# Gated linear attention: decays to the chunks' ends taken in the exponential's bias, a subtraction taken into scans, and GpSimd's elementwise work moved to VectorE

## The chip, the cores and the metric

One core of a Trainium2 chip runs the whole program in one launch. The metric is device time in microseconds (us) from the first to the last instruction of an execution; the time before is the median of three.

## What is computed

Two transformer blocks on 256 tokens of width 1024 in fp32. The first block has three token mixers on one input projection (attention, gated linear attention, a Hyena convolution) and a mixture of experts; the second has four feed-forward layers, a pooling mixer and a sparse attention. The change lies in the gated linear attention (four heads, chunks of 64 tokens, a forward and a backward direction), and in one line of the convolution:

```python
def gla_log_decay(a_low, w_a2, b_a):
    z = (a_low @ w_a2 + b_a)
    return to_heads(jax.nn.log_sigmoid(z) / GLA_TAU, GLA_HEADS)          # GLA_TAU = 16

def gla_chunked(q, k, v, log_a, s0):             # latent tokens, per chunk of 64
    cum = jnp.cumsum(log_a, axis=3);  cum_last = cum[:, :, :, -1:, :]
    q_dec = q * jnp.exp(cum);         k_inv = k * jnp.exp(-cum)
    k_to_end = k * jnp.exp(cum_last - cum)
    att = where(tril, q_dec @ k_inv.T, 0);       o_intra = att @ v
    chunk_state = k_to_end.T @ v;                chunk_decay = jnp.exp(cum_last)
    # states are scanned over the chunks; o = o_intra + q_dec @ state

def gla_final_state(k, v, log_a):                # context tokens, one run of 256
    cum = jnp.cumsum(log_a, axis=2)
    return jnp.einsum('bhld,bhlv->bhdv', k * jnp.exp(cum[:, :, -1:, :] - cum), v)
```

The context's final state is the latent tokens' first one. The backward direction is the same on flipped tokens.

## The kernel before

**Layout.** Every head has one tile of 128 partitions by 512 columns: the forward direction's 64 key channels are partitions 0 to 63 (`lo`), the backward's 64 to 127 (`hi`); columns 0 to 255 are the latent tokens, 256 to 511 the context's. The work order on every engine is a scheduler's, made from the order in which the code records it and its priorities; each engine then runs its own list in order. PE's list runs almost without a break, since the split matmuls of the projections (`in_tiles`, L1354) make up most of the work: each tile is 24 matmuls (`mm3`, lines 169, 171, 173), for which ScalarE rounds the weights (`wh`, line 158) and VectorE subtracts the rest (`wl`, line 159), three tiles ahead at most.

**`Gla.decays` (L645).** A generator that `in_tiles` steps between the projection's tiles. Per head a matmul (L659), then ScalarE's absolute value and exponential into a tile `e` of the ring `L2` (four buffers; L662, L663), and VectorE's minimum with zero into `cum` (L664). After the last of these ScalarE takes the logarithm ln(1+e) of all four heads (L669), GpSimd subtracts it from `cum` (L671), and VectorE makes running sums in place: two scans for the latent tokens, which restart at the chunks (L674, L676, times the mask `seg`), and two for the context (L678, L680).

**`hyena` (L540).** The convolution runs in the same stretch. Its transposes (L570) are split by ScalarE and VectorE into `zt` (`E.split`, lines 158 and 159), which PE's transforms read; VectorE multiplies the results with the spectra (L582 to L586), GpSimd combines them (L584, L587), and PE's inverse transform (L592) waits for that.

**`Gla.mix` (L683).** Per head VectorE forms `df`, the difference from each chunk's end: L700 for the latent tokens, L701 for the context, each once per direction. ScalarE exponentiates it (L706), GpSimd multiplies it with the keys `kd` (L710), PE transposes it (L713), and products with the values follow (L719, L724). ScalarE's exponentials L704 and L705 and VectorE's products L708 and L709 make queries and inverse keys; L729 and L731 chain the states; L738 masks; L743 and L746 are the output's matmuls; L747 copies it. At this time the attention's query tiles still come through `in_tiles`: ScalarE squares and copies each (L816, L817), VectorE and GpSimd rotate it (L771 to L774), and PE sums the squares (L810).

Of the kernel before, what the change touches and what calls it, by code (L numbers as in the profile page):

```python
# [13 lines left out]
AF = mybir.ActivationFunctionType  # L14
OP = mybir.AluOpType
# [4 lines left out]
T = 256  # L20
# [519 lines left out]
def hyena(E, W, VI, hp, qs, spec, in_tiles, yh, yl):  # L540

    nc = E.nc
    V = nc.vector
    G = nc.gpsimd
# [19 lines left out]
    for o in range(2):  # L564
        sp = spec[o]
        zt = [hp.t([128, 2, 512], f"zt{i}", 1, FR) for i in range(2)]
        for t in range(2):
            ps = E.mx()
            for c in range(4):
                nc.tensor.transpose(ps[:, 128 * c : 128 * c + 128], z[:, c, 128 * t : 128 * t + 128], E.ident)  # L570
            E.split(zt[0][:, t], zt[1][:, t], ps)
        yield
        y = hp.t([128, 4, 512], "hyy")
        for m in range(2):
            zr = E.mx()
# [24 lines left out]
class Gla:  # L600
# [44 lines left out]
    def decays(self, qs):  # L645


        E, VI, ga = self.E, self.VI, self.ga
        nc = E.nc
        A = nc.scalar.activation  # L650
        V = nc.vector
        wa = E.const("gla_wa", qs)
        seg = E.const("seg", qs)
        lo, hi = slice(0, 64), slice(64, 128)
        self.cum = cums = qs.t([128, 4, 512], "cum")
        es = []
        for h in range(4):
            ps = E.mx()
            nc.tensor.matmul(ps, wa[:, 128 * h : 128 * h + 128], ga, start=True, stop=True)  # L659
            b = VI["gla_ba"][:, h : h + 1]  # L660
            e = E.l2()
            A(e, ps, AF.Abs, bias=b)  # L662
            last = A(e, e, AF.Exp, scale=-1.0).ins  # L663
            V.tensor_scalar(cums[:, h], ps, b, 0.0, OP.add, OP.min)  # L664
            es.append(e)
            yield
        with E.tc.issue_after(last):
            for h in range(4):
                A(es[h], es[h], AF.Ln, bias=1.0)  # L669
        for h in range(4):  # L670
            nc.gpsimd.tensor_sub(cums[:, h], cums[:, h], es[h])  # L671
        for h in range(4):
            cum = cums[:, h]
            V.tensor_tensor_scan(cum[lo, :T], seg[lo], cum[lo, :T], 0.0, OP.mult, OP.add)  # L674
            yield
            V.tensor_tensor_scan(cum[hi, :T][:, ::-1], seg[hi, ::-1], cum[hi, :T][:, ::-1], 0.0, OP.mult, OP.add)  # L676
            yield
            V.tensor_tensor_scan(cum[lo, T:], cum[lo, T:], cum[lo, T:], 0.0, OP.add, OP.bypass)  # L678
            yield
            V.tensor_tensor_scan(cum[hi, T:][:, ::-1], cum[hi, T:][:, ::-1], cum[hi, T:][:, ::-1], 0.0, OP.add, OP.bypass)  # L680
            yield

    def mix(self, gp, yh, yl):  # L683
        E, VI, ga, kd, gv, qd, sog = self.E, self.VI, self.ga, self.kd, self.gv, self.qd, self.sog
        nc = E.nc
        A = nc.scalar.activation
        V = nc.vector
        G = nc.gpsimd
# [5 lines left out]
        lo, hi = slice(0, 64), slice(64, 128)  # L694
        for h in range(4):
            cum = self.cum[:, h]
            df = E.l2()
            for s, l, lc in ((lo, 63, 511), (hi, 0, 256)):
                cl = cum[s, l : T : 64].unsqueeze(2).to_broadcast([64, 4, 64])
                V.tensor_sub(df[s, :T].rearrange("a (c t) -> a c t", c=4), cl, cum[s, :T].rearrange("a (c t) -> a c t", c=4))  # L700
                V.tensor_scalar(df[s, T:], cum[s, T:], cum[s, lc : lc + 1], -1.0, OP.subtract, OP.mult)  # L701
            ec = gp.t([128, T], "g_ec", 2)
            ei = gp.t([128, T], "g_ei", 2)
            A(ec, cum[:, :T], AF.Exp, scale=1.0 / 16)  # L704
            A(ei, cum[:, :T], AF.Exp, scale=-1.0 / 16)  # L705
# [1434 lines left out]
```

## Time and profile before

| | |
|---|---|
| runs | 1712.97, 1717.15, 1720.77 us; median 1717.15 |
| profiled execution | 1721.04 us; its span 1719.3 us |
| PE busy, of the span | 1651.5 us, 96% |
| VectorE, ScalarE, GpSimd busy | 998.1, 775.6 and 145.4 us |
| mean granted TensorE clock | 0.975 |

The span begins at the first instruction of any engine. Shares over the whole span average stages with different limits, so the stretches in which PE is not busy, or its granted clock is low, are looked at by themselves. [...]

### The profile page before, as it was taken

How to read it: one execution, taken by the hardware profiler on the slowest of the kernel's cores; microseconds unless marked ns; L12 is line 12 of the kernel's file. 1: busy time of each engine (PE TensorE's matmuls, PEld its weight loads, DVE VectorE, ACT ScalarE, POOL GpSimd, SP SyncE). 2: the span in 40 equal slices, each digit the busy share in tenths (PEclk: the TensorE clock that was granted, in tenths of full speed). 3: DMA queues.
4: the chain of work that ended last, by engine and by line, in shares of the span. 5: the costliest groups of instructions: out<-in, count | busy, mean ns of one | idle time of the engine just before them, and what ended most of it. 6: DMA issues, size and time to landing. Idle time of an engine off the chain costs nothing.

```text
span 1719.3 us, 24121 instructions
## 1 busy us (share of the span) xinstructions
PE 1651.5 (96%) x9266; PEld 1286.0 (75%) x9266; DVE 998.1 (58%) x2034; ACT 775.6 (45%) x1616; POOL 145.4 (8%) x149
## 2 busy tenths in 40 slices
PE   6999898899989999989999999999999998999998
PEld 3777787799975444358888688888888897788886
DVE  4635869786552323156654666547555686885544
ACT  3533344365441001045544555436554575865442
POOL 1001215111120000020000000000000022300000
PEclk8999998999999999999999899999999998999999
DMA  9454353137537999956454454555455351065450
GB/s 361 165 185 164 126 169 124 62 99 296 182 145 309 426 425 426 426 227 225 171 188 167 176 190 165 187 193 205 176 182 184 137 198 58 22 257 200 169 190 33
DMA packets 60380, 343.39 MB, mean 200 GB/s; under 512 B 7329, under 2 KB 8161, under 8 KB 28769
## 3 DMA queue, kind: packets, MB, share of 16 engines
q1 hardware_dynamic: 57680, 333.29, 52.0%
q0 software_dynamic: 1776, 6.56, 1.1%
q10 hardware_dynamic: 800, 1.92, 0.3%
q8 instruction: 75, 1.23, 0.3%
q14 instruction: 49, 0.39, 0.1%
HBM read 340.69 MB, written 1.05 MB: 199 GB/s over the span
## 4 chain that ended last, share of the span: by engine, by line
PE 53%; DVE 1%; ACT 1%; DMA 0%; POOL 0%; issue 0%; DVEq 0%; POOLq 0%; ACTq 0%
PE mm L169 16%; PE mm L171 15%; PE mm L173 15%; PE mx L1658 1%; PE mx L1995 1%; PE mx L1507 1%; PE acc L2042 1%; PE mm L2022 1%; PE mm L1754 0%; DMA c_pool_b<-in_pool_b_dram 0%; PE mm L1752 0%; PE mm L1745 0%; PE acc L2031 0%; PE mx L1820 0%; PE acc L2035 0%
## 5 line engine op out<-in xcount | busy, mean ns | idle before, releaser
L159 DVE TENSOR_TENSOR wl<-wr,wh 128x512 fp32r<-128x512 f32 x768 | 498.4, 700 | 237.9 <-ACT wh L158 224.5
L158 ACT ACTIVATE wh<-wr 128x512 fp32r<-128x512 f32 x768 | 428.6, 622 | 307.2 <-PE mm L173 183.1
L169 PE MATMUL mm<-wh,xh 128*128 128x512 f32 (+1 forms) x752 | 204.0, 393 | 0.0
L173 PE MATMUL mm<-wh,xl 128*128 128x512 f32 (+1 forms) x752 | 198.6, 386 | 0.0
L171 PE MATMUL mm<-wl,xh 128*128 128x512 f32 (+1 forms) x752 | 198.2, 386 | 0.0
L173 PEld LDWEIGHTS mm<-wh,xl 128*128 128x128 f32 x752 | 139.1, 188 | 28.7
L171 PEld LDWEIGHTS mm<-wl,xh 128*128 128x128 f32 x752 | 139.1, 188 | 28.6
L169 PEld LDWEIGHTS mm<-wh,xh 128*128 128x128 f32 x752 | 136.1, 188 | 26.1 <-ACT xh L1519 0.4
L1138 PE MATMUL mm<-wr,xg 128*64 128x512 f32 x512 | 124.9, 596 | 0.0
L171 PE MATMUL mm<-wl,hidh 128*128 128x512 f32 x352 | 98.6, 396 | 0.0
L173 PE MATMUL mm<-wh,hidl 128*128 128x512 f32 x352 | 98.0, 396 | 0.0
L169 PE MATMUL mm<-wh,hidh 128*128 128x512 f32 x352 | 97.7, 395 | 0.0
L1650 DVE SCALAR_TENSOR_TENSOR L<-mm,r,L 128x256 f32<-128x256 f32 x88 | 42.5, 483 | 92.8 <-ACT L L1649 90.3
L1649 ACT ACTIVATE L<-mm,r 128x256 f32<-128x256 f32 x88 | 41.8, 475 | 117.5 <-PE mm L173 115.1
L1138 PEld LDWEIGHTS mm<-wr,xg 128*64 128x64 f32 x512 | 37.4, 137 | 67.3 <-issue 64.6
L173 PEld LDWEIGHTS mm<-wh,hidl 128*128 128x128 f32 x352 | 66.1, 188 | 15.8
L171 PEld LDWEIGHTS mm<-wl,hidh 128*128 128x128 f32 x352 | 65.9, 188 | 15.9
L169 PEld LDWEIGHTS mm<-wh,hidh 128*128 128x128 f32 x352 | 65.8, 188 | 15.6
L169 PE MATMUL mm<-hh,wh 128*128 128x256 f32 x480 | 75.1, 295 | 0.0
L173 PE MATMUL mm<-hh,wl 128*128 128x256 f32 x480 | 71.5, 288 | 0.0
L169 PEld LDWEIGHTS mm<-hh,wh 128*128 128x128 f32 x480 | 65.3, 195 | 7.7 <-issue 3.3
L171 PE MATMUL mm<-hl,wh 128*128 128x256 f32 x480 | 70.6, 287 | 0.0
(589 smaller groups left out, 2370.7 us busy)
## 6 DMA issues: line engine op xcount, KB each, us to landing
wr<-in_ffn_in_dram SPq DMA_DIRECT2D x88, 1024.0 KB, 4.8
wr<-in_moe_in_dram SPq DMA_DIRECT2D x64, 1024.0 KB, 12.7
wr<-in_ffn_out_dram SPq DMA_DIRECT2D x40, 1024.0 KB, 4.9
wr<-in_moe_out_dram SPq DMA_DIRECT2D x32, 1024.0 KB, 15.1
wr<-in_w_in_f_dram SPq DMA_DIRECT2D x55, 512.0 KB, 4.1
wr<-in_w_mod_dram SPq DMA_DIRECT2D x48, 512.0 KB, 6.1
wr<-in_nsa_in_f_dram SPq DMA_DIRECT2D x8, 1024.0 KB, 4.7
wr<-in_w_br_att_dram SPq DMA_DIRECT2D x8, 512.0 KB, 3.2
```

What stands on the lines that cost most here:

```text
L158: self.nc.scalar.activation(hi, src, AF.Copy)
L159: (eng or self.nc.vector).tensor_sub(lo, src, hi.bitcast(F32))
L169: nc.tensor.matmul(ps, lhs[0][k], rhs[0][k], start=first and k == 0, stop=False)
L171: nc.tensor.matmul(ps, lhs[0][k], rhs[1][k], start=False, stop=False)
L173: mm = nc.tensor.matmul(ps, lhs[1][k], rhs[0][k], start=False, stop=last and k == kt - 1)
L1138: PE.matmul(ps[s], x[:, s], w, start=start, stop=stop)
L1507: E.nc.tensor.transpose(tp[:, 128 * j : 128 * j + 128], self.x[:, t, c : c + 128], E.ident)
L1649: A(s, ps[:, :T], AF.Silu, scale=r)
L1650: V.scalar_tensor_tensor(h, ps[:, T:], r, s, OP.mult, OP.mult)
L1658: PE.transpose(tp[:, 256 * j + 128 * t : 256 * j + 128 * t + 128], hs[n, t][:, 128 * j : 128 * j + 128], E.ident)
L1995: PE.matmul(dst, qs[:, h // 2, h % 2, q], part[:, h // 4, :, : n // 2], start=t == 1 and i == 0, stop=t == 0 and i == 1 and j == 1)
L2022: PE.transpose(tp[:, 128 * j : 128 * j + 128], probs(u)[:, 128 * j : 128 * j + 128], E.ident)
```

## The change

- **Decays.** The logarithm is written in two halves of 256 columns: the latent tokens' in place, the context's to a tile `rest` (tag `sog`, whose place the query projection takes later). The subtraction of the latent half goes from GpSimd to VectorE; that of the context's half is taken into its two scans, whose second operand is now `rest` with a subtraction. The generator yields 8 times in its scan part where it yielded 16 times. Four small operations then write a sixteenth of the running sums at the chunks' ends (four chunks and the context) to a new tile `ends`.
- **Mix.** The differences L700 and L701 and the exponential L706 over 512 columns are replaced by five exponentials per head on `cum` itself, four over 64 columns and one over 256, with `ends` as the bias. The product with the keys goes from GpSimd to VectorE.
- **Hyena.** The split of the transposes is recorded with high priority.

```diff
@@ hyena @@
-            E.split(zt[0][:, t], zt[1][:, t], ps)
+            with E.tc.high_priority():
+                E.split(zt[0][:, t], zt[1][:, t], ps)
@@ Gla.decays @@
+        rest = qs.t([128, 4, T], "sog")
         with E.tc.issue_after(last):
             for h in range(4):
-                A(es[h], es[h], AF.Ln, bias=1.0)
+                A(es[h][:, :T], es[h][:, :T], AF.Ln, bias=1.0)
+                A(rest[:, h], es[h][:, T:], AF.Ln, bias=1.0)
+                V.tensor_sub(cums[:, h, :T], cums[:, h, :T], es[h][:, :T])
         for h in range(4):
-            nc.gpsimd.tensor_sub(cums[:, h], cums[:, h], es[h])
-        for h in range(4):
-            cum = cums[:, h]
+            cum, ex = cums[:, h], rest[:, h]
             V.tensor_tensor_scan(cum[lo, :T], seg[lo], cum[lo, :T], 0.0, OP.mult, OP.add)
-            yield
...
-            V.tensor_tensor_scan(cum[lo, T:], cum[lo, T:], cum[lo, T:], 0.0, OP.add, OP.bypass)
+            V.tensor_tensor_scan(cum[lo, T:], cum[lo, T:], ex[lo], 0.0, OP.add, OP.subtract)
...
+        self.ends = ends = qs.t([128, 4, 5], "ends")
+        for s, l, lc in ((lo, 63, 511), (hi, 0, 256)):
+            V.tensor_scalar_mul(ends[s, :, :4], cums[s, :, l : T : 64], 1.0 / 16)
+            V.tensor_scalar_mul(ends[s, :, 4:], cums[s, :, lc : lc + 1], 1.0 / 16)
@@ Gla.mix, per head @@
-            for s, l, lc in ((lo, 63, 511), (hi, 0, 256)):
-                cl = cum[s, l : T : 64].unsqueeze(2).to_broadcast([64, 4, 64])
-                V.tensor_sub(df[s, :T].rearrange(...), cl, cum[s, :T].rearrange(...))
-                V.tensor_scalar(df[s, T:], cum[s, T:], cum[s, lc : lc + 1], -1.0, OP.subtract, OP.mult)
+            for c in range(5):
+                q = slice(64 * c, 64 * c + 64 if c < 4 else 512)
+                A(df[:, q], cum[:, q], AF.Exp, scale=-1.0 / 16, bias=self.ends[:, h, c : c + 1])
...
-            A(df, df, AF.Exp, scale=1.0 / 16)
...
-            G.tensor_mul(df, kd[:, h], df)
+            V.tensor_mul(df, kd[:, h], df)
```

PE's list and SP's list of loads have the same rows in the same order before and now. GpSimd's list loses the four subtractions L671 and the four products L710, and its two later splits of queries (line 159 on `ga` and `c_gla_wa`) move behind the sixth rotation (they stood behind the first and the second).

VectorE's list up to the first two `zt` splits, before (a scan is listed as SCALAR_TENSOR_TENSOR; the first row is the first head's last scan, the second one of the second head, and `qT` with 255 columns is the convolution of an input tile):

```order
L680 SCALAR_TENSOR_TENSOR cum_1498<-cum_1498 64x256
L674 SCALAR_TENSOR_TENSOR cum_1498<-c_seg_1496,cum_1498 64x256
L556 SCALAR_TENSOR_TENSOR qT_1456<-mm_1651,c_vec_11_98,qT_1456 128x255
L159 TENSOR_TENSOR wl_1811<-wr_1809,wh_1812 128x512
L557 SCALAR_TENSOR_TENSOR qT_1456<-mm_1651,c_vec_11_98,qT_1456 128x255
L159 TENSOR_TENSOR wl_1811<-wr_1809,wh_1812 128x512
L159 TENSOR_TENSOR wl_1876<-wr_1874,wh_1877 128x512
L556 SCALAR_TENSOR_TENSOR qT_1456<-mm_1696,c_vec_11_98,qT_1456 128x255
L159 TENSOR_TENSOR wl_1876<-wr_1874,wh_1877 128x512
L557 SCALAR_TENSOR_TENSOR qT_1456<-mm_1696,c_vec_11_98,qT_1456 128x255
L159 TENSOR_TENSOR zt_272_1734<-mx_1735,zt_271_1733 128x512
L159 TENSOR_TENSOR zt_272_1734<-mx_1742,zt_271_1733 128x512
```

And now, up to the same two `zt` splits (L674 is the latent subtraction, L677 and L678 the latent scans, L680 and L681 the context scans, `sog` is `rest`):

```order
L674 TENSOR_TENSOR cum_1498<-cum_1498,L_253_1591 128x256
L678 SCALAR_TENSOR_TENSOR cum_1498<-c_seg_1496,cum_1498 64x256
L681 SCALAR_TENSOR_TENSOR cum_1498<-cum_1498,sog_1679 64x256
L556 SCALAR_TENSOR_TENSOR qT_1456<-mm_1651,c_vec_11_98,qT_1456 128x255
L674 TENSOR_TENSOR cum_1498<-cum_1498,L_260_1639 128x256
L557 SCALAR_TENSOR_TENSOR qT_1456<-mm_1651,c_vec_11_98,qT_1456 128x255
L677 SCALAR_TENSOR_TENSOR cum_1498<-c_seg_1496,cum_1498 64x256
L678 SCALAR_TENSOR_TENSOR cum_1498<-c_seg_1496,cum_1498 64x256
L159 TENSOR_TENSOR wl_1819<-wr_1817,wh_1820 128x512 x2
L556 SCALAR_TENSOR_TENSOR qT_1456<-mm_1702,c_vec_11_98,qT_1456 128x255
L159 TENSOR_TENSOR zt_273_1741<-mx_1742,zt_272_1740 128x512
L159 TENSOR_TENSOR zt_273_1741<-mx_1749,zt_272_1740 128x512
```

The two `zt` splits stood behind the `wl` splits of two tiles; now they stand behind those of one, but, counted from the first of either list, behind six scans and four subtractions where it was five scans.

ScalarE, where the query tiles are squared and copied, before (`L` rows from L706 are the exponentials of the second to fourth head):

```order
L706 ACTIVATE L_430_2833<-L_430_2833 128x512
L158 ACTIVATE wh_3063<-wr_3060 128x512 x2
L816 ACTIVATE hyy_2398<-mm_2623 128x256
L817 ACTIVATE qT_2395<-mm_2623,c_vec_11_98 128x256
L706 ACTIVATE L_443_2890<-L_443_2890 128x512
L706 ACTIVATE L_456_2947<-L_456_2947 128x512
L158 ACTIVATE wh_3097<-wr_3094 128x512 x2
L816 ACTIVATE hyy_2398<-mm_2673 128x256
L817 ACTIVATE qT_2395<-mm_2673,c_vec_11_98 128x256
L158 ACTIVATE wh_3131<-wr_3128 128x512 x2
L816 ACTIVATE hyy_2398<-mm_2713 128x256
L817 ACTIVATE qT_2395<-mm_2713,c_vec_11_98 128x256
```

And now, from the first of the new exponentials (L820 and L821 are the former L816 and L817):

```order
L706 ACT_TABLE_LOAD
L706 ACTIVATE L_419_2786<-cum_1498,ends_2114 128x64 x2
L158 ACTIVATE wh_2628<-wr_2625 128x512 x2
L820 ACTIVATE hyy_2410<-mm_2505 128x256
L821 ACTIVATE qT_2407<-mm_2505,c_vec_11_98 128x256
L706 ACTIVATE L_419_2786<-cum_1498,ends_2114 128x64 x2
L706 ACTIVATE L_419_2786<-cum_1498,ends_2114 128x256
L706 ACTIVATE L_432_2843<-cum_1498,ends_2114 128x64
L158 ACTIVATE wh_2678<-wr_2675 128x512 x2
L820 ACTIVATE hyy_2410<-mm_2545 128x256
L821 ACTIVATE qT_2407<-mm_2545,c_vec_11_98 128x256
L706 ACTIVATE L_432_2843<-cum_1498,ends_2114 128x64 x3
```

There are eight query tiles. Before, the first exponential stood behind the fourth tile's copy and the last two behind the sixth's, each ahead of weight roundings and of the seventh tile's squares. Now the first stands behind the second tile's copy and the last ahead of the sixth tile's squares.

## Rows read from the trace of the kernel before

**Rows 1.** The page: busy time of every engine over the span, and two rows of its 40 slices of 43 us each (busy tenths of VectorE, and granted TensorE clock in tenths).
```profile
PE 1651.5 (96%) x9266; PEld 1286.0 (75%) x9266; DVE 998.1 (58%) x2034; ACT 775.6 (45%) x1616; POOL 145.4 (8%) x149
...
DVE  4635869786552323156654666547555686885544
...
PEclk8999998999999999999999899999999998999999
```

**Rows 2.** Windows: a stretch in us from the span's start, its length, then busy us (and instructions) of PE, weight loads, VectorE, ScalarE and GpSimd, the granted clock as a share of 2.4 GHz, the DMA engines' busy share and GB/s.
```profile
178.44:184.57 6.13, 6.13 (x52) 5.15 (x51) 6.06 (x5) 5.50 (x12) 4.50 (x3) 1.00 0.00 0
...
184.57:189.50 4.93, 0.00 (x1) 0.01 (x1) 4.93 (x11) 0.21 (x1) 0.00 (x0) 0.83 0.31 91
...
189.50:194.60 5.10, 5.10 (x13) 3.96 (x14) 4.73 (x9) 0.00 (x0) 0.00 (x0) 0.50 0.68 243
...
194.60:206.00 11.40, 10.78 (x73) 8.86 (x72) 11.30 (x16) 3.21 (x6) 5.66 (x4) 1.00 0.37 130
...
262.00:282.24 20.24, 20.24 (x173) 20.15 (x171) 19.66 (x31) 10.98 (x22) 12.21 (x14) 1.00 0.44 142
...
282.24:286.67 4.43, 0.00 (x1) 0.01 (x1) 4.30 (x7) 2.00 (x5) 2.83 (x3) 0.64 0.04 15
...
286.67:303.50 16.83, 14.24 (x67) 13.19 (x67) 14.88 (x35) 6.06 (x15) 6.88 (x10) 0.60 0.33 109
...
303.50:340.00 36.50, 32.22 (x262) 28.35 (x262) 28.08 (x68) 11.96 (x22) 6.20 (x3) 0.99 0.17 59
...
480.00:500.00 20.00, 20.00 (x143) 16.28 (x141) 8.52 (x16) 11.09 (x24) 6.27 (x6) 1.00 0.00 1
...
520.00:760.00 240.00, 234.41 (x1120) 103.45 (x1120) 64.50 (x148) 29.88 (x58) 7.31 (x7) 0.99 0.90 377
```

**Rows 3.** Waits of PE from 173 to 345 us: what waited, for which engine and line, us in total, times, longest.
```profile
PE mx L171 <- DVE zt L159: 4.9, 1, 4.9
...
PE mx L810 <- ACT hyy L816: 4.4, 1, 4.4
...
PE mx L737 <- DVE g_ei L709: 1.5, 1, 1.5
...
PE mx L592 <- POOL hyy L587: 0.5, 1, 0.5
```

**Rows 4.** The order of time from 175 to 190 us, ScalarE, GpSimd, VectorE and PE: start, us, engine, line, operation, out<-in, shape; in brackets the idle time before it and what ended it.
```profile
176.40 2.19 ACT L669 ACTIVATE L<-L 128x512 f32<-128x512 f32 x4
...
177.12 5.82 POOL L671 TENSOR_TENSOR cum<-cum,L 128x512 f32<-128x512 f32 x4 [27.55 <-ACT L L669]
...
178.44 1.77 DVE L674 TENSOR_TENSOR_SCAN cum<-c_seg,cum 64x256 f32<-64x256 f32 x1 [3.24 <-POOL cum L671]
...
180.22 1.62 DVE L676 TENSOR_TENSOR_SCAN cum<-c_seg,cum 64x256 f32<-64x256 f32 x1
...
181.85 1.63 DVE L678 TENSOR_TENSOR_SCAN cum<-cum 64x256 f32<-64x256 f32 x1
...
183.49 0.69 DVE L680 TENSOR_TENSOR_SCAN cum<-cum 64x256 f32<-64x256 f32 x1
...
188.77 1.27 DVE L159 TENSOR_TENSOR zt<-mx,zt 128x512 fp32r<-128x512 f32 x2
...
189.50 1.40 PE L171 MATMUL mx<-zt,ft 128*128 128x512 f32 x2 [4.93 <-DVE zt L159]
```

**Rows 5.** Groups of instructions from 262 to 290 us, shapes apart: busy us, mean ns of one | idle us before, and what ended it.
```profile
L159 DVE TENSOR_TENSOR wl<-wr,wh 128x512 fp32r<-128x512 f32 x11 | 8.3, 773 | 0.2
...
L700 DVE TENSOR_TENSOR L<-cum 64x256 f32<-64x256 f32 x8 | 6.8, 852 | 0.1
...
L701 DVE TENSOR_SCALAR L<-cum 64x256 f32<-64x256 f32 x8 | 6.1, 758 | 0.1
...
L706 ACT ACTIVATE L<-L 128x512 f32<-128x512 f32 x4 | 2.5, 631 | 10.0 <-DVE L L701 10.0
...
L710 POOL TENSOR_TENSOR L<-kd,L 128x512 f32<-128x512 f32 x4 | 5.7, 1418 | 1.6 <-ACT L L706 1.6
```

**Rows 6.** The order of time from 278 to 305 us, some rows of ScalarE, then PE, then VectorE; columns as in Rows 4.
```profile
284.68 0.63 ACT L706 ACTIVATE L<-L 128x512 f32<-128x512 f32 x1 [3.51 <-DVE L L701]
...
286.25 0.36 ACT L816 ACTIVATE hyy<-mm 128x256 f32<-128x256 f32 x1
...
286.67 1.01 PE L810 MATMUL mx<-mean,hyy 128*128 128x1 f32 x4 [4.43 <-ACT hyy L816]
...
301.46 0.63 PE L743 MATMUL mx<-at,gv 128*128 128x128 f32 x2
...
296.87 0.27 DVE L726 COPY g_sp<-mx 64x128 f32<-64x128 f32 x1
...
299.77 0.78 DVE L738 COPY_PREDICATED at<-c_gla_mask,mx 128x256 f32<-128x256 uint32 x2
```

**Rows 7.** Groups of instructions, shapes apart: three of ScalarE before 760 us, and one of VectorE from 175 to 212 us.
```profile
L1240 ACT ACTIVATE cs<-c_vec 128x16 f32<-128x16 f32 x1 | 0.2, 232 | 0.0
...
L704 ACT ACTIVATE g_ec<-cum 128x256 f32<-128x256 f32 x4 | 1.6, 410 | 2.1 <-DVE g_sp L731 1.3 <-PE mx L810 0.8
...
L988 ACT ACTIVATE xa<-xT,a 128x256 f32<-128x256 f32 x8 | 4.0, 495 | 0.0
...
L594 DVE TENSOR_TENSOR uc<-uc,qT 128x256 f32<-128x256 f32 x1 | 0.4, 393 | 0.0
```

More of the change, by code (lines that the diff above doesn't have):

```diff
@@ L666, in decays @@
             yield
+        rest = qs.t([128, 4, T], "sog")
         with E.tc.issue_after(last):
             for h in range(4):
-                A(es[h], es[h], AF.Ln, bias=1.0)
+                A(es[h][:, :T], es[h][:, :T], AF.Ln, bias=1.0)
+                A(rest[:, h], es[h][:, T:], AF.Ln, bias=1.0)
+                V.tensor_sub(cums[:, h, :T], cums[:, h, :T], es[h][:, :T])
         for h in range(4):
-            nc.gpsimd.tensor_sub(cums[:, h], cums[:, h], es[h])
-        for h in range(4):
-            cum = cums[:, h]
+            cum, ex = cums[:, h], rest[:, h]
             V.tensor_tensor_scan(cum[lo, :T], seg[lo], cum[lo, :T], 0.0, OP.mult, OP.add)
-            yield
             V.tensor_tensor_scan(cum[hi, :T][:, ::-1], seg[hi, ::-1], cum[hi, :T][:, ::-1], 0.0, OP.mult, OP.add)
             yield
-            V.tensor_tensor_scan(cum[lo, T:], cum[lo, T:], cum[lo, T:], 0.0, OP.add, OP.bypass)
+            V.tensor_tensor_scan(cum[lo, T:], cum[lo, T:], ex[lo], 0.0, OP.add, OP.subtract)
+            V.tensor_tensor_scan(cum[hi, T:][:, ::-1], cum[hi, T:][:, ::-1], ex[hi, ::-1], 0.0, OP.add, OP.subtract)
             yield
-            V.tensor_tensor_scan(cum[hi, T:][:, ::-1], cum[hi, T:][:, ::-1], cum[hi, T:][:, ::-1], 0.0, OP.add, OP.bypass)
-            yield
+        self.ends = ends = qs.t([128, 4, 5], "ends")
+        for s, l, lc in ((lo, 63, 511), (hi, 0, 256)):
+            V.tensor_scalar_mul(ends[s, :, :4], cums[s, :, l : T : 64], 1.0 / 16)
+            V.tensor_scalar_mul(ends[s, :, 4:], cums[s, :, lc : lc + 1], 1.0 / 16)
     def mix(self, gp, yh, yl):
@@ L697, in mix @@
             df = E.l2()
-            for s, l, lc in ((lo, 63, 511), (hi, 0, 256)):
-                cl = cum[s, l : T : 64].unsqueeze(2).to_broadcast([64, 4, 64])
-                V.tensor_sub(df[s, :T].rearrange("a (c t) -> a c t", c=4), cl, cum[s, :T].rearrange("a (c t) -> a c t", c=4))
-                V.tensor_scalar(df[s, T:], cum[s, T:], cum[s, lc : lc + 1], -1.0, OP.subtract, OP.mult)
+            for c in range(5):
+                q = slice(64 * c, 64 * c + 64 if c < 4 else 512)
+                A(df[:, q], cum[:, q], AF.Exp, scale=-1.0 / 16, bias=self.ends[:, h, c : c + 1])
             ec = gp.t([128, T], "g_ec", 2)
```

## The prediction

> **What bounds the kernel now.** The page first: PE is busy for 96% of the span, and its list is unchanged, so the change can only matter where PE is not busy or not at full clock. The slice from 258 to 301 us is such a place: VectorE at nine tenths, the clock at eight; the one from 172 us has VectorE at eight [rows 1]. The chain of waits, which would be read next, says nothing here: it starts at 754 us, behind a branch. So the stretches were cut into windows. Two of them show the same picture, VectorE full and PE empty: from 184.57 to 189.50 PE does nothing and VectorE is busy for all 4.93 us; from 282.24 to 286.67 PE does nothing and VectorE is busy for 4.30 of 4.43 us. Behind each of them the granted clock is low: 0.50 for 5.1 us behind the first, 0.60 on average over 16.83 us behind the second [rows 2]. That is the 1.2 GHz level for all, then for most of these windows; the clock fell in the course of each wait. The list of PE's waits names who was late: the `zt` split (4.9 us) and ScalarE's squares L816 (4.4 us) [rows 3]. These two are by far the longest of the stretch.
>
> Why they were late is read from the order of time. **First wait:** the four GpSimd subtractions L671 run from 177.12 for 5.82 us. VectorE's first scan begins only at 178.44, and its first three take 1.77, 1.62 and 1.63 us; the fourth, which runs when GpSimd has finished, takes 0.69. Then follow the work of two tiles, and the `zt` splits start at 188.77 [rows 4]. **Second wait:** ScalarE runs in order, and its last exponential L706 starts at 284.68 after 3.51 us of waiting for VectorE's L701; the squares L816 that PE wants come behind it at 286.25 [rows 6]. In total ScalarE waited 10.0 us for L701 there [rows 5].
>
> **The change part by part, at the first wait.** GpSimd's four subtractions go. ScalarE's first logarithm of 256 columns would end some 0.41 us (a 256-column activation [rows 7]) after 176.40 [rows 4], so VectorE begins at about 176.8 and not at 178.4: 1.6 us gained. Three scans lose what they had more than 0.69 us: 5.02 - 2.07 = 2.95 us gained. Four subtractions of 256 columns are added, bounded by 0.39 us for such a product alone [rows 7] and 0.45 us with hand-over: 1.7 us lost. The context's subtraction inside the scan is not in the trace; a scan over two different tiles (L674 has `seg` and `cum`) takes what one over one tile takes, since the three long ones, of both kinds, are within 0.15 us of each other [rows 4]; I take 0.69 us, with 0 and 0.3 us each as the bounds. Up to the two splits there are by list two 0.7 us halves of `wl` fewer and one scan more: 0.6 us gained. Sum: 1.6 + 2.95 - 1.7 + 0.6 = 3.5 us. The eight halves of logarithms take ScalarE up to 8 x 0.41 - 2.19 = 1.1 us longer, but the `zt` copy stays ahead of VectorE, which reaches it at about 185.3. PE's wait would shrink to about 1.5 us, and the short waits for GpSimd behind it, in the window from 194.6, ran at 1.00 [rows 2, 3]. The clock's part is 5.1 us at 1.2 GHz, worth 2.5 us if PE alone set the pace; but VectorE is full there too (11.30 of 11.40 us [rows 2]), so I count nothing of it. The four operations that write `ends` have 16 columns and fewer, so each costs less than the 0.39 us of 256 [rows 7]; they stand behind all scans, where PE is busy again: nothing, or 1.6 us of VectorE's slack. I take **3 us**; bounds 0 (the `wl` pushed back behind `zt` are now the late ones) and 6 (3.5 + 2.5).
>
> **At the second wait.** VectorE loses L700 and L701, 6.8 + 6.1 = 12.9 us, and gets four products of 128x512. Their price is bounded by 0.64 us (half of the pair of `zt` splits of that size [rows 4]) and GpSimd's own 1.42; the nearest is a `wl` split in this stretch, 0.77, two SBUF inputs of the same size [rows 5]: 3.1 us. So VectorE has about 10 us less to do, in a window where it had 19.66 of 20.24 us [rows 2], and is no longer behind. ScalarE's exponentials need only `cum` and `ends`, which the first stretch leaves behind, so it waits for nobody. Its own load rises: 16 activations of 64 columns and 4 of 256, all with a bias pointer. The trace has none of 64; 16 columns take 0.23 us and 256 with two pointers 0.50, against 0.41 without [rows 7]. I take 0.34 for 64 columns and 0.48 for 256, together 7.4 us against 2.5 before; with 10.98 us of 20.24 before [rows 2] that leaves it under 16 us. `wh` is prepared three tiles ahead, so PE doesn't see that.
>
> So the 4.43 us go. What comes next is the first head. PE's work from 286.67 to the output's L743 at 301.46 [rows 6] is 12.2 us at mostly half clock, in a window that was busy for 14.24 of 16.83 us at 0.60 [rows 2]; at full clock it is some 6 to 7 us. The chain through VectorE is the longer one. The sums and transposes that took from 286.67 to 289 at half clock end at about 284.6, if they begin at 282.24. Then come two exponentials of 256 columns (0.41 each [rows 7]) and the copy of the transposes (512 columns, as L706 0.63 [rows 5]) on ScalarE, about 1 us of PE's small products, and VectorE's states and mask, 3.7 us from 296.87 to the end of the mask's 0.78 us at 299.77 [rows 6]. 284.6 + 1.4 + 1 + 3.7 is 290.7, and with hand-overs 292: **9.5 us** earlier than 301.46. Half a microsecond more comes from the matmuls behind that which ran at 1.2 GHz. The later three heads ran at full clock with their own short waits, and keep them.
>
> [...]
>
> Does the gain reach the end? Between 480 and 500 us the DMA engines move 1 GB/s: all loads ahead are in, and the experts' weights (377 GB/s from 520 on) start as PE frees places [rows 2]. So all behind moves up. **Sum: 3 + 9.5 + 0.5 = 13 us.** The profiled execution, 1721.04 us, would become 1708; it is 3.9 us above the median of the runs, 1717.15, so the forecast for a median is **1704**.
>
> **Rivals.** (1) *The clock stays low anyway.* From 281.3 PE has only the squares' sums (one column each) and transposes, then the first head with its short waits. For it: a mean of 0.64 over the wait of 4.43 us means 1.2 GHz for the last 3.2 us, so the clock fell only 1.2 us into the wait, and it stayed low over the first head, although PE was busy for 14.24 of 16.83 us. Against it: the sums of the first tiles lie in a window at 1.00, and the later heads, with short waits, in one at 0.99 [rows 2]. Then only the wait's 4.43 us go, less 2 that the half clock hides, and with 2.5 to 3 us of the first wait it is 5 us: 1712. [...] (2) *The gain is given back* at a transfer or a fixed delay behind: 1717. Against it is the row of 480 us. (3) *Slower: ScalarE becomes the late one.* The new exponentials stand ahead of the weight roundings and squares of four query tiles, some 13.5 us of PE's work. ScalarE's other work in them is 13.5 / 20.24 of 10.98 - 1.9 us, 6 us. If 64 columns cost as much as 256 with two pointers, 0.50 us, the exponentials add 10 us: ScalarE is 2.5 us late at 275, and if the three tiles' lead is used up, PE waits for `wh`, and runs the tiles up to 282 at half clock, 7 us more; the first head gains nothing, as before. 2.5 + 7 - 4.4 for the old wait - 3 at the first stretch is 2 us slower, and 3 us more if the first stretch gains nothing: 1722. It decides from 0.37 us each, where the four tiles are just full; 0.23 for 16 columns and the lead speak against it. That the change doesn't do what it says is excluded by the lists.
>
> **How the numbers follow.** Forecast 0.62, clock 0.20, given back 0.09, slower 0.09. A measurement can tell about 0.5%, 8.6 us. The forecast's own bounds are 0 + 9 = 9 us and 6 + 12.5 = 18.5 us, so it counts as faster; cases 1 and 2 are the same. The range reaches from 1698 to 1715: it takes in case 1 and leaves out case 3 and most of case 2.
>
> **What would show it.** Right: PE's wait for `zt` under 2 us and none for L820 (the former L816); the first three scans at 0.7 us; a clock of 1.00 from 186 to 300; VectorE busy for under 13 of the 20 us from 262; L743's first group some 12 us earlier than 301.46. Wrong: a clock of 0.5 behind 281 without a wait, ScalarE waits turned into PE waits for `wh` from 265 on, or PE waits for `wl` at 190.

## The result and the profile after

The changed kernel takes 1708.33 us (median of 8 runs, 1707.97 to 1709.71), the kernel before 1717.65 us (8 runs, 1712.97 to 1720.77): a ratio of 0.9948, interval 0.9937 to 0.9960. The time lies in the range of the prediction (1698 to 1715) and moved the way that was forecast; the gain of 9.3 us is 3.7 us short of the 13 that were forecast. The profiled execution took 1707.97 us, with a span of 1706.2.

The page after, as in [rows 1]: busy time of every engine, then the 40 slices of VectorE and of the granted clock.

```profile
PE 1648.7 (97%) x9266; PEld 1283.1 (75%) x9266; DVE 988.4 (58%) x2030; ACT 778.7 (46%) x1636; POOL 136.0 (8%) x141
...
DVE  4645968795642222265545566557555685886544
...
PEclk9999999999999999999999899999999998999999
```

GpSimd has 8 instructions fewer and ScalarE 20 more. In the slice from 256 us the clock is at nine tenths where it was at eight; VectorE is at eight there, and at nine in the slice from 171. Line numbers have shifted: L659 is now L660, L671 L674, L592 L593, L584 L585, L710 L714, L816 L820, L743 L747. In the changed kernel L816 is another line, VectorE's copy of the squares' sums (`ssq`).

PE's waits from 170 to 345 us, the answer to [rows 3]:

```profile
PE mx L593 <- POOL hyy L585: 3.0, 1, 3.0
PE mx L261 <- DVE bd L203: 2.6, 2, 1.8
PE mx L741 <- DVE g_ei L713: 1.5, 1, 1.5
PE mx L747 <- DVE at L742: 1.4, 3, 0.6
PE mx L728 <- DVE wl L159: 1.3, 1, 1.3
PE mx L741 <- DVE g_sp L731: 1.0, 1, 1.0
PE mx L171 <- DVE zt L159: 0.7, 1, 0.7
PE mx L593 <- POOL hyy L588: 0.5, 1, 0.5
```

Both long waits are gone (4.9 for `zt` is 0.7; the 4.4 for the squares is not in the list). The first line is new: PE waits 3.0 us for GpSimd's combination L585, where it waited 0.4 us for the same one (then L584) before; the wait for the second combination, 0.5 us, is as it was.

The order of time from 172 to 199 us, VectorE, GpSimd and PE (start, us, engine, line; in brackets the idle time before), the answer to [rows 4]:

```profile
172.79 0.42 DVE L674 TENSOR_TENSOR cum<-cum,L 128x256 f32<-128x256 f32 x1 [1.64 <-ACT L L672]
...
173.13 0.68 DVE L680 TENSOR_TENSOR_SCAN cum<-cum,sog 64x256 f32<-64x256 f32 x1
...
180.49 1.28 DVE L159 TENSOR_TENSOR zt<-mx,zt 128x512 fp32r<-128x512 f32 x2
...
187.51 1.29 POOL L585 TENSOR_TENSOR hyy<-hyy,L 128x512 f32<-128x512 f32 x1 [42.00 <-DVE L L584]
...
187.87 1.48 DVE L677 TENSOR_TENSOR_SCAN cum<-c_seg,cum 64x256 f32<-64x256 f32 x1
...
194.79 0.68 DVE L584 TENSOR_TENSOR L<-mx,spec 128x512 f32<-128x512 f32 x1
...
195.55 1.26 POOL L585 TENSOR_TENSOR hyy<-hyy,L 128x512 f32<-128x512 f32 x1 [5.11 <-DVE L L584]
196.09 1.26 DVE L681 TENSOR_TENSOR_SCAN cum<-cum,sog 64x256 f32<-64x256 f32 x1
196.77 1.65 POOL L588 TENSOR_TENSOR hyy<-hyy,L 128x512 f32<-128x512 f32 x1
196.86 1.13 PE L593 MATMUL mx<-wr,hyy 128*128 128x256 f32 x4 [2.99 <-POOL hyy L585]
```

A scan takes 0.68 us with GpSimd idle. Beside L585 scans take 1.48 and 1.26 again: the stretching that [rows 4] shows has moved down the list. The second L585 starts as soon as VectorE's L584 is done, and PE stands until it is done.

Windows after, the answer to [rows 2] (stretch, length, busy us of PE, weight loads, VectorE, ScalarE, GpSimd, then the granted clock and DMA):

```profile
195.00:200.00 5.00, 2.66 (x10) 2.04 (x11) 4.94 (x6) 0.00 (x0) 2.87 (x2) 0.86 0.00 1
200.00:205.00 5.00, 5.00 (x34) 4.38 (x34) 4.92 (x10) 1.60 (x3) 0.00 (x0) 0.79 0.43 129
262.00:282.00 20.00, 18.52 (x156) 17.99 (x155) 19.42 (x35) 13.22 (x37) 13.59 (x15) 1.00 0.41 136
280.00:285.00 5.00, 2.37 (x14) 1.94 (x14) 4.70 (x14) 0.00 (x0) 2.65 (x4) 0.90 0.47 161
285.00:290.00 5.00, 5.00 (x24) 4.95 (x24) 3.46 (x9) 2.26 (x5) 0.00 (x0) 0.50 0.00 0
290.00:301.00 11.00, 10.37 (x87) 9.40 (x87) 8.34 (x24) 4.81 (x9) 2.29 (x1) 0.96 0.15 51
```

From 262 to 282 VectorE is busy for 19.42 of 20 us: it was not relieved. PE's clock still falls, behind the new wait (0.86, 0.79) and behind the short waits of the first head (0.50 for the whole of 285 to 290), but the second time for some 7 us (the 5 us of that row, 1 us by the mean of 0.90 before it and 0.9 by the 0.96 behind it) and not for some 17, which is what 0.64, 0.60 and 0.99 in [rows 2] come to.

**Where the time went.** The two profiles cannot be laid on each other as they are: the changed kernel's first L660, ahead of all that was changed, is at 155.0 us, and the first L659 before at 159.1. So everything below is counted from that instruction. The columns are the last start of the inverse transform (L592, L593), the first start of the output's L743 (L747), and the last start of the experts' first product (L1138, L1142 into `mm`), all in us from there, each from one profile. Ratios are against the kernel before on the same chip.

| kernel | inverse transform ends | first L743 | experts end | time | ratio, 95% |
|---|---|---|---|---|---|
| before | 95.5 | 142.4 | 567.1 | 1717.65 | |
| changed | 93.5 | 132.8 | 557.8 | 1708.33 | 0.9948 (0.9937 to 0.9960) |
| before again (e1) | 95.6 | 142.4 | 567.3 | 1718.99 | |
| second part alone (e2) | 95.6 | 134.2 | 560.3 | 1713.43 | 0.9971 (0.9959 to 0.9983) |
| first part alone (e3) | 93.3 | 140.0 | 564.6 | 1715.14 | 0.9982 (0.9972 to 0.9992) |
| no priority (e4) | 93.0 | 132.4 | 557.0 | 1707.41 | 0.9942 (0.9928 to 0.9955) |
| roots in one chain (e5) | 93.3 | 131.3 | 557.2 | 1706.49 | 0.9931 (0.9911 to 0.9950) |
| rotations on VectorE (e6) | 93.4 | 128.9 | 551.8 | 1700.79 | 0.9895 (0.9870 to 0.9920) |
| combinations on VectorE (e7) | 89.3 | 127.9 | 552.0 | 1704.20 | 0.9927 (0.9907 to 0.9947) |
| product on GpSimd (e8) | 93.1 | 133.9 | 559.6 | 1710.30 | 0.9956 (0.9944 to 0.9969) |
| e6 and e7 together (e9) | 89.2 | 124.7 | 547.9 | 1699.15 | 0.9888 (0.9872 to 0.9905) |
| e4, e5, e6, e7 together (e10) | 89.3 | 124.8 | 547.4 | 1699.09 | 0.9893 (0.9876 to 0.9910) |
| e6 and e7 without the change (e11) | 93.3 | 135.5 | 561.6 | 1713.82 | 0.9977 (0.9965 to 0.9990) |

The first stretch gains 2.0 us (3 forecast), the second 7.6 (10 forecast), and 9.3 arrive at the experts' end: the measured gain. The intervals of e4, e5, e7 and e8 overlap that of the changed kernel, so what is said of them below rests on the marks.

The first stretch had more in hand at first. The inverse transform's matmuls before and after, with their first and last start:

```profile
L592 PE MATMUL mx<-wr,hyy x64: 377/379/483, 203.6 to 254.6; 128*128 128x256 f32 x64
L593 PE MATMUL mx<-wr,hyy x64: 377/379/653, 193.3 to 248.5; 128*128 128x256 f32 x64
```

From the first L659 or L660 the first of them starts at 44.5 us before and at 38.3 after, 6.2 us earlier; 2.0 of these are left at the last.

### The profile page after: what moved, and what is told of

It is laid out like the page before. It is cut to its first block, busy times and chain, and to the rows that moved or that the text cites. A ratio compares the mean times of both kernels' runs of the same rounds, so it can differ in the third digit from the quotient of the medians.

```text
span 1706.2 us, 24125 instructions
## 1 busy us (share of the span) xinstructions
PE 1648.7 (97%) x9266; PEld 1283.1 (75%) x9266; DVE 988.4 (58%) x2030; ACT 778.7 (46%) x1636; POOL 136.0 (8%) x141
## 4 chain that ended last, share of the span: by engine, by line
PE 54%; DVE 1%; DMA 1%; ACT 1%; POOL 0%; issue 0%; DVEq 0%; POOLq 0%; ACTq 0%
PE mm L169 16%; PE mm L171 16%; PE mm L173 16%; PE mx L1662 1%; PE mx L1999 1%; PE mx L1511 1%; PE acc L2046 1%; PE mm L2026 1%; PE mm L1758 0%; DMA wr<-in_ffn_in_dram 0%; DMA c_pool_b<-in_pool_b_dram 0%; PE mm L1756 0%; PE mm L1749 0%; PE acc L2035 0%; PE mx L1824 0%; PE acc L2039 0%
## 5 line engine op out<-in xcount | busy, mean ns | idle before, releaser
L171 PE MATMUL mm<-wl,xh 128*128 128x512 f32 (+1 forms) x752 | 198.2, 386 | 0.0
L171 PEld LDWEIGHTS mm<-wl,xh 128*128 128x128 f32 x752 | 139.1, 188 | 28.6
L1142 PE MATMUL mm<-wr,xg 128*64 128x512 f32 x512 | 124.9, 596 | 0.0
L171 PE MATMUL mm<-wl,hidh 128*128 128x512 f32 x352 | 98.6, 396 | 0.0
L1142 PEld LDWEIGHTS mm<-wr,xg 128*64 128x64 f32 x512 | 37.4, 137 | 67.3 <-issue 64.6
L171 PEld LDWEIGHTS mm<-wl,hidh 128*128 128x128 f32 x352 | 65.9, 188 | 15.9
L171 PE MATMUL mm<-hl,wh 128*128 128x256 f32 x480 | 70.7, 287 | 0.0
## 6 DMA issues: line engine op xcount, KB each, us to landing
wr<-in_moe_in_dram SPq DMA_DIRECT2D x64, 1024.0 KB, 12.9
```

The lines of the kernel that those rows point to most:

```text
L171: nc.tensor.matmul(ps, lhs[0][k], rhs[1][k], start=False, stop=False)
L1142: PE.matmul(ps[s], x[:, s], w, start=start, stop=stop)
```

## The experiments

The theory: GpSimd and VectorE hold each other up, so the time that the removed operations took beside GpSimd was GpSimd's and fell to the next ones. What the rows show of it is longer operations on both. A scan takes 0.67 to 0.69 us with GpSimd idle, 1.62 to 1.77 beside its subtractions [rows 4] and 1.26 to 1.63 beside its combinations in the changed kernel. GpSimd's product of a rotation there (L777) takes 0.73 us at the shortest, and 1.18 at 265, 269 and 272 us, where VectorE is full. How one engine holds up the other no run shows: GpSimd's hold, below, is the time by which VectorE's operations are longer beside it. The rivals are named with each run.

**e1: the kernel before, unchanged, profiled again.**

> The kernel before, unchanged, profiled once more. In the two profiles at hand the changed kernel is already 4.05 us earlier where nothing was changed (the first L659, now L660, at 159.1 us before and at 155.0 after). Theory: that is a difference between executions in the transfers of the start, and no work of the change: here the first L659 comes anywhere from 154 to 159 us, and from there on the second profile shows the stretches of the first again within 1 us (first L743 142.4 us behind the first L659, VectorE's first three scans of L674 and L676 at 1.6 to 1.8 us each, PE's waits of 4.9 us for zt and of 4.4 us for L816). Rival: the start belongs to the kernel (the scheduler's order): the first L659 is at 159 us again, within 0.5 us, and 4 of the 13.1 us between the two profiles come from the change.

The first L659 came at 156.5 us and not at 159.1, and from there on all three marks agree within 0.2 us. Over all 13 profiles of this record it lies between 155.0 and 160.2 us, with the change in the kernel and without it. Of the 13.1 us between the spans of the two profiles, about 4 are a difference between executions.

**e2 and e3: each part alone.**

```diff
 # e2: the kernel before, with ends behind the scans and the changed mix; e3: the changed kernel with
 # the old mix and without ends
-            V.tensor_sub(df[s, :T] ...); V.tensor_scalar(df[s, T:] ...); A(df, df, AF.Exp, ...); G.tensor_mul(df, kd[:, h], df)
+            for c in range(5): A(df[:, q], cum[:, q], AF.Exp, scale=-1.0 / 16, bias=self.ends[:, h, c : c + 1])
+            V.tensor_mul(df, kd[:, h], df)
```

> Only the second part of the change: the decays as before (subtraction and zt order too), then ends, and mix as changed. Theory: the two parts hold in their own places and add up. The first stretch is as before (PE waits 4.9 us for zt); the second loses its wait of 4.4 us, and the first group of L743 comes 7.6 us earlier, net of all that lies ahead: 1710.3 us, 7.3 us under the kernel before. Rival 1 (VectorE is full in the second stretch with or without the change, so the second stretch gains only because the first hands it work earlier): the wait for the squares stays at over 2 us, and the gain is 3 us or less: 1715. Rival 2 (the first part brings nothing by itself): all of the 9.3 us are here: 1708.3.

> Only the first part of the change: zt first, subtraction on VectorE, context's subtraction inside the scans; mix as before (differences on VectorE, product on GpSimd), no ends. Theory: the first stretch is as in the changed kernel (wait for zt 0.7 us, a new wait of 3 us of the inverse transform for GpSimd's hyy), so that 2.05 us are left at its end; the second stretch still has its wait of 4.4 us for the squares: 1715.6 us, 2 us under the kernel before. [...] Rival 2 (the second wait gives all of it back): 1717.6.

The parts keep to their places. Two waits of PE with the first part alone:

```profile
PE mx L811 <- ACT hyy L817: 4.3, 1, 4.3
PE mx L593 <- POOL hyy L585: 2.9, 1, 2.9
```

The second stretch's wait stands as before; the new one of the first is there. With the second part alone it is the other way: PE waits 4.9 us for `zt`, and no longer for the squares. By the marks e3 gains 2.5 us and e2 6.8, together the 9.3 of the whole; by the times 2.5 and 4.2, with intervals of 1.4 to 4.8 and 2.9 to 7.0. That the first part alone brings nothing, or shortens the second wait, is excluded. The time of e2, 1713.43, lies between the theory's 1710.3 and the 1715 of its rival 1; its waits and marks are the theory's.

**e4: the changed kernel without the priority of `zt`.**

```diff
-            with E.tc.high_priority():
-                E.split(zt[0][:, t], zt[1][:, t], ps)
+            E.split(zt[0][:, t], zt[1][:, t], ps)
```

> The changed kernel without the priority of the zt split. Theory: the splits are reached by VectorE one or two half-width ops later, since the long wait went with GpSimd's subtractions and not with the order: PE's wait for zt 1.5 to 2.5 us in place of 0.72, scans at 0.7 us, and the inverse transform's wait for GpSimd takes up most of the difference: 1708.3 to 1709.3. Rival: the order is what removes the first wait: the wait for zt is 4 us or more again, and the 2 us of the first stretch are lost: 1710.3 or more.

The waits for `zt` sum to 1.2 us, less than the theory's 1.5 to 2.5, the inverse transform waits 2.6 for GpSimd, and all marks are 0.4 to 0.8 us earlier than with the priority. The first wait went with GpSimd's subtractions; the priority does nothing that these runs can tell.

**e5: the inverse roots of the attention's queries in one chain.**

```diff
-        for j in range(2):
-            m = ssq[:, 4 * j : 4 * j + 4]...;  E.rsqrt(m, 8, ...);  V.tensor_scalar_mul(rq[:, 4 * j : 4 * j + 4], ...)
+        m = ssq...;  E.rsqrt(m, 16, ...);  V.tensor_scalar_mul(rq, rq, 128 ** -0.5)
```

> The changed kernel with one more edit: the inverse roots rq of the attention's queries in one chain over 16 columns behind the last tile, not in two chains over 8. VectorE's list loses exactly the first chain (L196 to L203 and L839, 8 operations), which in the changed kernel's profile takes 5.0 us between 269.7 and 281.0, 3.1 of it between PE's sums and the copy L816 that frees the PSUM buffer on which PE waits 1.3 us in L728; all other lists are the same. Theory: in the stretch of the first head VectorE is still behind, and its list sets the pace: the wait of 1.3 us goes, that for g_ei (1.5 us) shrinks, the first group of L743 (L747) comes 3 us earlier than in the changed kernel, counted from the first L660, and the time is 1705.3 us. Rival: the first head is set by PE at 1.2 GHz and by ScalarE, and VectorE only looks busy: the group moves by under 1 us, 1707.5 or more.

Half of the theory's 3 us: L747 comes 1.5 us earlier, the experts' end 0.6. The wait of 1.3 us in L728 is gone, but that for `g_ei` grew from 1.5 to 2.5, because its product L713 now took 1.42 us beside a rotation (0.95 in the changed kernel, 0.42 in e6). With eight operations out of VectorE's list, GpSimd's hold fell on another one.

**e6: the rotations of the query tiles on VectorE.**

```diff
-        E.nc.gpsimd.tensor_mul(x, x, self.rc)
-        E.nc.gpsimd.tensor_add(x, x, tb)
+        (V or E.nc.gpsimd).tensor_mul(x, x, self.rc)        # V is VectorE for the eight query tiles
+        (V or E.nc.gpsimd).tensor_add(x, x, tb)
```

> The changed kernel with the two rotation operations of each of the eight query tiles (a product and a sum of 128x256) on VectorE in place of GpSimd. Theory: VectorE is full there because it and GpSimd shut each other out; without GpSimd the 14 splits wl go from 1.0 us back to 0.7 each and L198, L816 and L839 to 0.17, some 7 us, against 16 operations of 0.42 added, some 6.7: VectorE as full as before, with GpSimd nearly idle, and the time within 1.5 us of the changed kernel, 1707 to 1710. Rival (the stretch comes from VectorE's own queue and not from GpSimd): the splits stay at 1.0, the 6.7 us come on top, PE waits for VectorE in the query tiles: 1713 or more.

My theory was right on the splits and wrong on the time: I had expected no gain, and 6.0 us came at the experts' end (7.5 between the medians). Groups on VectorE in the stretch up to the sums' end, first of the changed kernel (257.9 to 281.1 us), then of this one (260.6 to 282):

```profile
L159 DVE TENSOR_TENSOR wl<-wr,wh 128x512 fp32r<-128x512 f32 x12 | 11.6, 1055 | 0.7 <-ACT wh L158 0.7
L714 DVE TENSOR_TENSOR L<-kd,L 128x512 f32<-128x512 f32 x4 | 2.8, 688 | 0.1
...
L839 DVE TENSOR_SCALAR rq<-rq 128x8 f32<-128x8 f32 x1 | 1.5, 1491 | 0.0
L816 DVE TENSOR_SCALAR ssq<-mx 128x8 f32<-128x8 f32 x2 | 0.9, 468 | 0.0
```

```profile
L159 DVE TENSOR_TENSOR wl<-wr,wh 128x512 fp32r<-128x512 f32 x11 | 7.5, 685 | 0.1
...
L778 DVE TENSOR_TENSOR qT<-qT,L 128x256 f32<-128x256 f32 x7 | 2.9, 417 | 0.0
L777 DVE TENSOR_TENSOR qT<-qT,c_rope_c 128x256 f32<-128x256 f32 x7 | 2.9, 416 | 0.0
L714 DVE TENSOR_TENSOR L<-kd,L 128x512 f32<-128x512 f32 x4 | 2.7, 685 | 0.0
```

The splits fall from 1.06 to 0.69 us, as the theory had it: 4.1 us less, against 5.8 for the 14 rotation operations. That shows longer operations beside GpSimd's; that the two shut each other out is more than it shows. Besides, the scheduler has made new orders. The roots' chain (L196 to L203, L839), 5.0 us in the changed kernel, stands behind the first head, where it is no longer in the way; e5, which takes it out and leaves GpSimd's work, gains 1.5 us at L747. And PE's list, the same in e4, e5, e7 and e8 as in the changed kernel, is another one here: in the first head matmuls of the projections (L171) stand between those of L741. And the clock, in windows of this kernel:

```profile
275.00:280.00 5.00, 5.00 (x46) 5.00 (x45) 4.94 (x10) 3.05 (x8) 2.54 (x4) 1.00 0.53 161
280.00:285.00 5.00, 5.00 (x37) 4.24 (x38) 4.72 (x16) 2.17 (x6) 0.00 (x0) 1.00 0.35 105
285.00:290.00 5.00, 4.96 (x44) 4.75 (x43) 4.03 (x11) 2.40 (x6) 0.00 (x0) 1.00 0.26 82
290.00:295.00 5.00, 5.00 (x45) 4.56 (x43) 4.75 (x14) 2.63 (x6) 0.00 (x0) 1.00 0.38 134
```

PE is busy throughout these windows and its clock stays at 1.00: the picture that the prediction had drawn for the change itself. What I missed in the size: I had added up VectorE's load, and not looked at which of its operations PE waits for in the first head. How much of the 6.0 us is GpSimd's hold and how much the new orders, this run can't tell.

**e7: the convolution's combinations on VectorE.**

```diff
-            G.tensor_sub(y[:, m], y[:, m], t1)
+            V.tensor_sub(y[:, m], y[:, m], t1)
-            G.tensor_add(y[:, 2 + m], y[:, 2 + m], t2)
+            V.tensor_add(y[:, 2 + m], y[:, 2 + m], t2)
```

> The changed kernel with the eight combinations L585 and L588 of hyy (128x512) on VectorE in place of GpSimd. Theory: the new wait of the first stretch (3.0 us of L593 for L585, 0.5 for L588) comes from GpSimd's 1.27 and 1.66 us in a chain behind four products, while the scans and wl beside them are stretched by as much as the operations would take on VectorE (0.68 each): the wait shrinks to under 2 us and the end of the inverse transform comes about 1 us earlier, 1707.3 us. Rival (VectorE's queue is the bound of that stretch, and the combination is late because VectorE reaches L584 late): 2.7 us more on VectorE per filter push the second zt and the products back, the end comes 1 us or more later: 1709.5 or more.

The order of time from 190 to 198 us, VectorE and PE:

```profile
190.99 0.67 DVE L677 TENSOR_TENSOR_SCAN cum<-c_seg,cum 64x256 f32<-64x256 f32 x1
...
191.68 0.69 DVE L678 TENSOR_TENSOR_SCAN cum<-c_seg,cum 64x256 f32<-64x256 f32 x1
...
196.18 0.68 DVE L585 TENSOR_TENSOR hyy<-hyy,L 128x512 f32<-128x512 f32 x1
...
196.91 1.56 PE L593 MATMUL mx<-wr,hyy 128*128 128x256 f32 x6 [1.13 <-DVE hyy L585]
```

The wait is 1.1 us, the scans are back at 0.68, the clock is 1.00 from 175 to 205 us, and the inverse transform ends 4.2 us earlier than in the changed kernel: four times what I expected, since the half clock behind the wait goes as well. Counted from the first L660, the second L585 starts at 39.3 us and not at 40.5, and takes 0.68 us and not 1.26: both VectorE's relief and the faster operation bring L593 forward. The rival, that more work in VectorE's queue makes the end later, falls. At the experts' end it is 5.8 us; where the 1.6 beyond the first stretch come from is not shown.

**e8: the keys' product back on GpSimd.**

```diff
-            V.tensor_mul(df, kd[:, h], df)
+            G.tensor_mul(df, kd[:, h], df)
```

> The changed kernel with the product L714 of the keys back on GpSimd, as before the change. Theory (each GpSimd operation holds up VectorE's for as long): VectorE loses 4 operations of 0.69 us, GpSimd gets 4 of 1.3, VectorE stays full, the time is within 1 us: 1707.5 to 1709.5. Rival 1 (what counts is VectorE's own work, as in the prediction's sum): the first head comes up to 2.8 us earlier: 1706 or less. Rival 2: GpSimd's queue of rotations makes the product late for the transposes L717: a new wait of PE of 1 us or more for GpSimd there, 1711 or more.

1.8 us later at the experts' end, 2.0 by the medians: later than the theory or rival 1 allowed, though by 0.8 us only. No wait for GpSimd at L717 appeared (rival 2); PE waits 1.7 us for VectorE's copy L816 and 2.6 for its product `g_ei`. VectorE's two products of the rotation (L775, L776) now take 0.75 and 0.67 us from 255 to 285 us, in place of 0.48 and 0.42. Here PE's list is the changed kernel's, so by the marks the product's 0.69 us on VectorE cost the kernel less than the same product on GpSimd.

**e9, e10, e11: both moves together, all edits together, and both moves without the change.**

> The changed kernel with both GpSimd parts on VectorE: the two rotation operations of the query tiles and the combinations L585 and L588 of hyy. In their own profiles these moves ended 6.0 and 5.8 us earlier than the changed kernel, counted from the first L660. Theory: they act in two stretches, and each takes away GpSimd's hold on VectorE in its own: they add up to 11 to 12 us, 1696.5 to 1698; TensorE's clock is 1.00 from 175 to 300 us, and the inverse transform's end comes 4 us, the first group of L747 8 us earlier than in the changed kernel. Rival: the second stretch has one place to give and both moves draw on it: 1700 or more.

> The kernel of both moves, without the zt split's priority and with the inverse roots in one chain of 16 columns. Theory: without GpSimd beside it the first chain of roots takes 8 operations of 0.17 us and not 5.0, and it stands before no wait of PE any more, so one chain in place of two brings under 0.5 us; the order of zt some 0.5 us: 1696 to 1697.5, not to be told from both moves alone. Rival: VectorE is still what the first head waits for, and each operation of its list counts: 1.5 us or more under both moves alone.

> The kernel before with the same two moves and without the change. Theory: GpSimd's subtractions and its product of the keys, which the change takes away, still stand beside VectorE there, and VectorE has the differences as well; the first wait (4.9 us for zt) is as it was, and in the second stretch 6.7 us of rotations are added to a VectorE that ScalarE's exponentials wait for: 1715 to 1719, so the moves are worth 11 us only behind the change. Rival: the moves are worth the same without the change, since only GpSimd's rotations and combinations hold VectorE up: 1706.

e9 is 9.9 us ahead of the changed kernel by the marks and 9.2 by the medians, of 11.8 that the two moves gave alone: mostly additive, less than expected, with 1699.15 us between the theory's 1698 and the rival's 1700. TensorE's clock is 1.00 from 175 to 295 us; the theory had it to 300. It beats both kernels, with a ratio of 0.9888. e10 is the same within the noise, so with both moves made, the roots' chain and the priority bring nothing that can be told. Without the change the two moves are worth 3.8 us (5.5 by the marks): the wait of 4.9 us for `zt` stays in e11, and the squares are still 1.4 us late. So the moves bring most behind the change, as expected, though 1713.82 us is better than the 1715 to 1719 that I had said.

## Why the prediction was right, and where it was off

**Right.** VectorE was what both stalls waited for, and taking GpSimd's subtractions and the differences away ended both. The second ended because ScalarE's exponentials no longer need VectorE, as the prediction said: ScalarE stood 10.0 us in front of L706 before [rows 5], and 0.0 now. The prices of the new operations were met: four subtractions of 0.41 us each (0.39 to 0.45 taken), a context scan with the subtraction inside at 0.67 (0.69), a product at 0.69 (0.77), and the exponentials with a bias pointer, of which 0.34 us for 64 columns and 0.48 for 256 were taken. Their groups on ScalarE from 255 to 290 us, columns as in [rows 5]:

```profile
L706 ACT ACTIVATE L<-cum,ends 128x64 f32<-128x64 f32 x16 | 4.5, 341 | 0.0
...
L706 ACT ACTIVATE L<-cum,ends 128x256 f32<-128x256 f32 x4 | 2.0, 500 | 0.0
```

VectorE began 1.5 us earlier (1.6). ScalarE was never late, so rival 3 had no ground: PE waited for no `wh`. The gain went through to the end (9.6 us at L747, 9.3 at the experts' end), which excludes rival 2. Of the signs named for being right two failed: the clock, and VectorE's load from 262 us on.

**First wait, 3 us forecast, 2.0 measured.** The chain up to `zt` held, and PE's wait there shrank to 0.7 and not to 1.5. Two steps failed, in opposite directions, so that 2.0 came near 3 partly by luck. The clock's part was put at nothing because VectorE was full there; but the clock no longer fell behind this wait. PE reached the inverse transform 6.2 us earlier, 4.2 by the shorter wait and 2.0 beyond it, where 5.1 us at a clock of 0.50 [rows 2] are gone (the prediction's 1.2 GHz; the profile gives the clock as a share, and no run shows a frequency): the clock is 1.00 from 175 to 195 us. The other step left the short waits for GpSimd behind it as they were: 0.9 us before, they became 3.5. The scans that no longer ran beside the subtractions ran beside the combinations instead, and PE, which now came earlier, waited for these. The clock fell behind that wait, for some 3.5 us by the two windows: 2.6 us of waiting and up to 1.7 of half clock took 6.2 back to 2.0. e7 shows the cause: without GpSimd there the 6.2 us stay, the upper bound of the sum (6).

**Second wait, 10 us forecast, 7.6 measured (8.2 in e2).** The failed step is "VectorE has about 10 us less to do". The 12.9 us of L700 and L701 were durations beside GpSimd. The shortest of them took 0.42 and 0.34 us, which makes 8 x 0.42 + 8 x 0.34 = 6.1 us of their own; less the products' 2.8 that is 3.3 us of relief. The other 6.8 I put down to GpSimd's hold, most of which passed to what stands there next. An estimate from back-to-back rows with GpSimd idle (in e6 0.64 us from one 128x512 to the next, 0.43 for 64x256, 0.2 for the small ones; 0.35 for L701 in the kernel before) puts VectorE's own work at 16.7 of 24.0 busy us before (262 to 286.67 us), 17.4 of 22.2 after and some 21 of 20.6 in e6 (the stretches of e6's groups): the hold is some 7, 5 and nothing. So VectorE was busy for 19.4 of 20 us and not for under 13, and the 4.43 us went all the same. What came short is the first head. PE's sums of the squares end at 277.3, which is 122.3 us behind the first L660. The prediction's 284.6 is 125.5 behind the first L659, or 123.5 with the 2.0 of the first stretch taken off, so up to here the change did 1.2 us better. From there to L743 (now L747) the sum had 7.4 us, and it took 10.4:

```profile
276.82 0.50 PE L814 MATMUL mx<-mean,hyy 128*128 128x1 f32 x4
...
287.77 0.63 PE L747 MATMUL mx<-at,gv 128*128 128x128 f32 x2
```

In between PE waits 1.3 and 1.5 us for VectorE, and the clock falls to 0.50 for some 7 us. That is a piece of rival 1, which had given the gain 5 us. That the clock stays low without such waits is not what e6 shows: there PE's one wait from 262 to 300 us is 0.8 us, and the clock is 1.00 from 205 to 305 us.

**Which operations were longer.** The four new products took 0.69 us each in the stretch with GpSimd's rotations. The splits beside them took 1.06, against 0.69 in e6 without the rotations, and the eight operations of the roots' chain 5.0 us together, against 0.16 or 0.17 each in e6. So VectorE's relief was not lost at the products, but at the splits and the small operations around them.

**Not shown.** Whether the hold or the changed orders of VectorE's and PE's lists give more of e6's gain, and with it that of e9 to e11; a kernel that keeps the orders and drops GpSimd's work was not run. Nor, in e7, how much is GpSimd's hold on VectorE and how much its slower combination.

## What to carry to other kernels

Before an operation's time is booked as saved, compare its mean with the shortest row of its group: what lies above that can belong to the engine beside it and fall to the next operation, as it did here (the splits took 1.06 us, and 0.69 in e6). When VectorE is full and GpSimd works beside it, small elementwise work can be cheaper on VectorE, even though VectorE is the full one: the rotations moved there gave 7.5 us between the medians (e6), the keys' product moved back cost 2.0 (e8). And after the longest wait is gone, look for who is second at the place where the engine now arrives early.

## What the runs showed of the hardware

An operation of 128x8, L839, which took 0.17 us later in the same profile, took 1.49 us while GpSimd issued a DMA and cleared two tiles; the operations behind it ended with it:

```profile
279.40 0.58 POOL L84 DMA_DIRECT2D c_gla_mask<-in_gla_mask_dram  x1
279.52 1.49 DVE L839 TENSOR_SCALAR rq<-rq 128x8 f32<-128x8 f32 x1
279.63 1.38 DVE L159 TENSOR_TENSOR wl<-wr,wh 128x512 fp32r<-128x512 f32 x1
279.98 1.00 POOL L698 MEMSET at<- 128x512 f32 x2
280.24 0.78 DVE L816 TENSOR_SCALAR ssq<-mx 128x8 f32<-128x8 f32 x1
```

In e6 the splits and rotations beside the same clearing took 0.69 and 0.42 us, as here,

```profile
277.88 1.00 POOL L698 MEMSET at<- 128x512 f32 x2
...
278.12 0.69 DVE L159 TENSOR_TENSOR wl<-wr,wh 128x512 fp32r<-128x512 f32 x1
```

and were not held, so not every operation is held up. Which ones are, and why, these runs do not show.
